# The output projection's last 1024 columns: a fourth pair by seven products, and the two token tiles moved into their seeded banks in a fixed order

## The chip, the cores and the metric

The kernel runs on one core of a Trainium2 chip. The metric is the device time of one execution in microseconds (us), the median of several runs. A core has five engines that work side by side and wait for one another through semaphores: TensorE (PE; its weight loads are listed as PEld), VectorE (DVE), ScalarE (ACT), GpSimd (POOL) and SyncE (SP), which here only issues transfers between device memory and the on-chip memory. TensorE adds its products up in accumulation banks, which VectorE and ScalarE read; a bank of 512 float32 columns by 128 rows is called a bank below.

## The reference, cut to what matters

One layer is computed (DEPTH is 1), for 256 tokens of width 2048, all in float32:

```python
h = rmsnorm(x, norm_g)
h, gate = adaln(h, c, ada_w, ada_b)          # shift, scale and gate from c
proj = h @ w_in                              # 2048 -> 4 x 4096
b_gate, c_gate, v, g = split(proj, 4)
u = causal_depthwise_conv(c_gate * v, conv_w)
y = b_gate * u * silu(g)                     # (256, 4096)
x = x + gate * (y @ w_out)                   # 4096 -> 2048
return rmsnorm(x, final_g)
```

The change concerns the product `y @ w_out`, 256 x 4096 times 4096 x 2048, and the gated residual and final norm behind it.

## The kernel before

**Precision.** Each float32 operand of a matmul is split in two parts: a high part, a cast made by ScalarE (`split_hi`, L352), and a low part, the rest, a subtraction made by VectorE (`split_lo`, L357). A product is then three matmuls, high x high, high x low and low x high (`triple`, L719). The 4096 rows of `w_out` are cut into 32 blocks of 128, taken two at a time: 16 *pairs*, numbered 0 to 15. The tokens are two *token tiles* of 128, t = 0 and 1. The split activations `y` stay on chip.

**Columns.** The 2048 output columns are done in two halves of 1024 (`columns`, L771), each in two blocks of W = 512. In a half, a pair is loaded as one tile of 128 x 2048 (1 MB, `load_o`) and used in one of two ways.

- A *direct* pair: 2 token tiles x 2 blocks of rows x 2 blocks of columns = 8 triples, 24 matmuls. It costs ScalarE one cast and VectorE one low part of 128 x 2048.
- A pair *by seven products* (`seven`, L736): the 2 x 2 x 2 block product in Winograd's form, 7 triples, 21 matmuls. Sums of the weight blocks are built on VectorE (L742, L744, L745), the raw blocks that are used are cast (L743) and their low part taken (L746), and the sums are split too (L352, L357). The matching sums of the activations (`forms`) were made earlier, for pairs 10 to 15 (`token_forms`), whether they are used once or twice. Four sums land in banks of their own (p1, p6 and the two of p75) and are put together after the last such pair (`gather`, L761 to L769).

In the first half all six pairs 10 to 15 go by seven products; in the second half three (10, 11, 12), between direct pairs. The list in the call sets the order of the pairs. Pairs 6 to 9 of the second half come last, in four pieces of a single block of columns: `LAST = (3, 4)` names two groups of four row blocks (pairs 6 and 7, pairs 8 and 9), first for columns 1024 to 1535 (the *third quarter*), then for columns 1536 to 2047 (the *fourth quarter*), 24 matmuls each.

**The seeded banks.** The fourth quarter's part that the pairs have summed up is moved before its end: for each token tile (L845 to L850) VectorE adds the bank and the gathered sums (L847), multiplies by the gate (L848) and adds the residual (L849), and ScalarE copies the result into another bank, `po[t]` (L850). The last two pieces of weights are multiplied by the gate before they are split (L862), so their products add straight onto the seeded bank: 48 matmuls, the last of the kernel. What follows for each token tile is a square with its sum (L877), a root (L818, with one load of ScalarE's function table), a reciprocal (L819), scalings on VectorE and ScalarE (L826, L824, L828) and four output transfers (L829). The sums of squares of the other columns (`part_sum`, L871 and L872) have to be there for the root.

**Buffers.** Three kinds of tiles of 128 x 2048 rotate over three places each: raw weights and weight sums (`raw_o`, `sums_o`), high parts (`hi`), low parts (`lo`). A pair by seven products takes two places of each kind in turn. A cast can start only when the matmuls that used the place three tiles ago are done, and a load is issued only when the last reader of its place is done: for a direct pair's tile that is its low part (L357), for a raw tile of the other form L746.

**Order.** The program is written as a plain sequence; a scheduler puts each engine's instructions into one queue, and an engine works through its queue strictly from front to back. `in_order()` pins the order of what is traced within it, `behind(ended)` puts instructions behind the last pinned ones. Around the change before, the order was left to the scheduler.

Of the kernel before, what the change touches and what calls it, by code (L numbers as in the profile page):

```python
# [11 lines left out]
ALU = mybir.AluOpType  # L12
# [7 lines left out]
TT = T // P  # L20
# [10 lines left out]
SLOT = 2048  # L31
# [86 lines left out]
def short_conv_layer(ctx: ExitStack, tc: tile.TileContext, x, c, norm_g, ada_w, ada_b, w_in, conv_w, w_out, final_g, out):  # L118
    nc = tc.nc
# [25 lines left out]
    def w_tile(kind, name, dtype=F32, i=None):  # L145

        if i is None:
            i = nth[kind] % 3
            nth[kind] += 1
        return wpool.tile([P, SLOT], dtype, tag=f"{kind}{i}", name=name, bufs=1)  # L150
# [9 lines left out]
    def raw_tile(name):  # L160
        return w_tile("raw", name)
# [3 lines left out]
    @contextmanager  # L165
    def in_order():

        traced = nc.cur_bb.bb.instructions
        n = len(traced)
        yield  # L170
        last = {}
        for ins in list(traced[n:]):
            if ins.engine in last:
                tc.add_manual_dep(ins, last[ins.engine], after, reason="in order")
            last[ins.engine] = ins.name
        ended.update(last)

    @contextmanager
    def behind(last):

        traced = nc.cur_bb.bb.instructions
        n = len(traced)
        yield
        for ins in list(traced[n:]):
            if ins.engine in last:
                tc.add_manual_dep(ins, last[ins.engine], after, reason="behind")
# [13 lines left out]
    ended = {}  # L200
# [75 lines left out]
    for t in range(TT):  # L276
        for dh in range(2):
# [3 lines left out]
            else:  # L281
                nc.vector.scalar_tensor_tensor(
                    out=junk[:, t], in0=xt[t][dh], scalar=1.0, in1=xt[t][dh], op0=ALU.mult, op1=ALU.mult,
# [60 lines left out]
    def hi_tile():  # L344
        return w_tile("hi", "hi", F32R)

    def lo_tile(lo_tag="lo"):
        return w_tile(lo_tag, "lo", F32R)

    def split_hi(raw, n, hi=None):  # L350
        hi = hi_tile() if hi is None else hi
        nc.scalar.copy(hi[:, :n], raw[:, :n])  # L352
        return hi

    def split_lo(raw, n, hi, lo_tag="lo", lo=None):
        lo = lo_tile(lo_tag) if lo is None else lo
        nc.vector.tensor_tensor(out=lo[:, :n], in0=raw[:, :n], in1=hi[:, :n].bitcast(F32), op=ALU.subtract)  # L357
        return hi, lo
# [13 lines left out]
    def split(raw, n, lo_tag="lo"):  # L372

        return split_lo(raw, n, split_hi(raw, n), lo_tag)
# [216 lines left out]
    def gate(dc):  # L591
        return gates[dc // 2][:, dc % 2, :]
# [36 lines left out]
    SEVEN = range(10, 16)  # L629
# [24 lines left out]
    for ct in range(NS, NCT, 2):  # L654
        for q in QUARTERS:
            bank = psum.tile([P, CT, T], F32, tag="mm", name="mm_b")[:, 0:2]
            col = q * E + ct * P
            for kp in range(0, KT, KP):
                raw = raw_tile("raw")
# [4 lines left out]
                hi, lo = split(raw, SLOT)  # L664
# [28 lines left out]
    W = 512  # L693
    big = hpool.tile([P, 3 * D + W], F32, tag="big", name="big")
    xr = big[:, 0 : TT * D].rearrange("p (t f) -> p t f", t=TT)
    fg = big[:, TT * D : 3 * D]
    u2 = big[:, 3 * D :]
    ends = [z.rearrange("p a b f -> p (a b f)").rearrange("p (h f) -> p h f", h=2) for z in zs]
# [11 lines left out]
    def load_o(raw, e0, ne, c0, n):  # L710
        nc.sync.dma_start(
            raw.rearrange("p (k f) -> p k f", k=ne),
            w_out[0, e0 * P : (e0 + ne) * P, c0 : c0 + n].rearrange("(k p) f -> p k f", p=P),
        )
# [9 lines left out]
    def gated(t, c0, n, src, pr, at):  # L724


        cs = slice(c0, c0 + n)
        r = xr[:, t, cs]
        g = gates[c0 // 1024].rearrange("p a f -> p (a f)")[:, c0 % 1024 : c0 % 1024 + n]
        nc.vector.tensor_tensor(out=pr, in0=src, in1=g, op=ALU.mult)  # L730
        nc.vector.tensor_tensor(out=r, in0=r, in1=pr, op=ALU.add)
        nc.scalar.activation(pr, r, AF.Square, scale=D**-0.5, accum_out=fsq[:, t, at : at + 1])
        nc.vector.tensor_tensor(out=r, in0=r, in1=fg[:, cs], op=ALU.mult)
# [37 lines left out]
    def columns(c0, order, sevens, bank, p1, p6, p75, whole, loads=None):  # L771


        for n, j in enumerate(order):
            raw = w_tile("raw" if n == 0 and c0 == 0 else "lo", "raw_o")
            load_o(raw, 2 * j, 2, c0, 2 * W)
            if loads:
                loads(n - 4)
            if j in sevens:
                seven(j, raw, bank, p1, p6, p75, j == sevens[0], j == sevens[-1])  # L780
                if j == sevens[-1]:
                    gather(p1, p6, p75)
                continue
            hi, lo = split(raw, SLOT, "raw")
            places = [(t, k, d) for t in range(TT) for k in range(2) for d in range(2)]
            if n == 0 and c0:
                places.sort(key=lambda p: p[2])
            for t, k, d in places:
                o = slice((k * 2 + d) * W, (k * 2 + d + 1) * W)
                triple(  # L790
                    bank(t, d), y_parts(2 * j + k, t), hi[:, o], lo[:, o],
                    n == 0 and k == 0, j == order[-1] and k == 1 and (whole or d == 1),
                )

    def extra_banks():
        return [psum.tile([P, W], F32, tag="sm", name="mm_1", bufs=2) for _ in range(2)]

    def wide_bank(name):
        return psum.tile([P, 2, W], F32, tag="mm", name=name)
# [7 lines left out]
    for t in range(TT):  # L807
        c = ends[t].rearrange("p h f -> p (h f)")
        nc.vector.tensor_tensor(out=c, in0=wide[t].rearrange("p h f -> p (h f)"), in1=c, op=ALU.add)
    for t in range(TT):  # L810
        c = ends[t].rearrange("p h f -> p (h f)")
# [3 lines left out]
    def finish(t):  # L815
# [15 lines left out]
    halves = [wide_bank("mm_o") for _ in range(2)]  # L831
    p75 = wide_bank("mm_7")
    LAST = (3, 4)
    po = extra_banks()
    columns(
        2 * W, (0, 1, 2, 10, 3, 13, 11, 4, 14, 12, 5, 15), SEVEN[0:3],
        lambda t, d: halves[d][:, t], *po, p75, False,
    )

    def out_mm(bank, t, ep, hi, lo):  # L840
        for i in range(EP):
            o = slice(i * W, (i + 1) * W)
            triple(bank, y_parts(ep * EP + i, t), hi[:, o], lo[:, o], False, ep == LAST[-1] and i == EP - 1)

    for t in range(TT):  # L845
        c = ends[t][:, 1]
        nc.vector.tensor_tensor(out=c, in0=halves[1][:, t], in1=c, op=ALU.add)  # L847
        nc.vector.tensor_tensor(out=c, in0=c, in1=gate(3), op=ALU.mult)  # L848
        nc.vector.tensor_tensor(out=c, in0=c, in1=xr[:, t, 3 * W : 4 * W], op=ALU.add)  # L849
        nc.scalar.copy(po[t], c)  # L850
    for ep in LAST:
        raw = w_tile("lo", "raw_o")
        load_o(raw, ep * EP, EP, 2 * W, W)
        hi, lo = split(raw, SLOT, "raw")
        for t in range(TT):
            out_mm(halves[0][:, t], t, ep, hi, lo)
    late = []
    for ep in LAST:
        raw = w_tile("lo", "raw_o")
        load_o(raw, ep * EP, EP, 3 * W, W)  # L860
        raw3 = raw.rearrange("p (k f) -> p k f", k=EP)
        nc.vector.tensor_tensor(out=raw3, in0=raw3, in1=gate(3).unsqueeze(1).to_broadcast([P, EP, W]), op=ALU.mult)  # L862
        hi, lo = split(raw, SLOT, "raw")
        out_mm(po[0], 0, ep, hi, lo)
        late.append((ep, hi, lo))
    for t in range(TT):
        c = ends[t][:, 0]
        nc.vector.tensor_tensor(out=c, in0=halves[0][:, t], in1=c, op=ALU.add)
        gated(t, 2 * W, W, c, c, 1)
        ps = part_sum[:, t : t + 1]  # L870
        nc.vector.reduce_sum(ps, fsq[:, t, 0:2], axis=mybir.AxisListType.X)  # L871
        nc.vector.tensor_scalar_add(ps, ps, EPS)  # L872
# [30 lines left out]
```

## Time and profile before

| | |
|---|---|
| time, median of 3 runs (lowest, highest) | 905.26 us (904.65, 905.49) |
| profiled execution: its own time | 905.34 us |
| its span, first to last instruction | 903.6 us |
| TensorE: matmuls busy, weight loads busy | 888.2 us (98%), 851.0 us (94%) |
| VectorE busy | 670.2 us (74%) |
| ScalarE busy | 482.4 us (53%) |
| GpSimd busy | 87.3 us (10%) |
| granted TensorE clock, mean | 0.998 |
| moved by the DMA engines | 235.01 MB, mean 260 GB/s |
| second half of the columns: first matmul | at 809.92 us |

Times in the profile are counted from the span's start. The span is a little shorter than the time of the execution, so a time read from the trace has to be carried over by differences. Matmuls are pipelined: a row's length is longer than the distance to the next matmul, and the distance is what counts. Rows of a time view give start, length, engine, line, operation, written tile <- read tiles, shape and count, and in brackets the idle time before with what ended it. Tiles are written without their number there.

### The profile page before, as it was taken

The numbers are of one execution on the slowest core, as the hardware profiler recorded it, in microseconds if no ns is written. First come the engines' busy times: TensorE is split into PE (matmuls) and PEld (weight loads), VectorE is DVE, ScalarE is ACT, GpSimd is POOL, SyncE is SP. The second block draws the span as 40 slices with busy tenths as digits, with TensorE's granted clock in tenths as the row PEclk, the third lists the DMA queues.
The fourth block names the chain that finished last, engine by engine and source line by source line (L and its number), as shares of the span: only waits on it lengthen the run. The fifth ranks groups of instructions, "written<-read, shape, count | busy, mean of one in ns | idle before, by whom it ended". The sixth has DMA issues, their size and how long they took to land.

```text
span 903.6 us, 16403 instructions
## 1 busy us (share of the span) xinstructions
PE 888.2 (98%) x7000; PEld 851.0 (94%) x7000; DVE 670.2 (74%) x661; ACT 482.4 (53%) x427; POOL 87.3 (10%) x95
## 2 busy tenths in 40 slices
PE   7999999999999999999999999999999999999996
PEld 4899999999999999999999999999999988888884
DVE  5889989888888867765875677565555578889685
ACT  6767866665548756644433434443434435544443
POOL 0000000000000132024324303320000000000000
PEclk9999999999999999999999999999999999999999
DMA  9999999999998587687988888866666486675652
GB/s 309 366 368 368 363 313 354 353 369 351 351 328 286 162 279 247 187 257 236 287 238 241 257 279 263 248 211 200 188 187 190 138 304 209 212 251 163 214 182 94
DMA packets 159594, 235.01 MB, mean 260 GB/s; under 512 B 6804, under 2 KB 105284, under 8 KB 159136
## 3 DMA queue, kind: packets, MB, share of 16 engines
q1 hardware_dynamic: 156384, 226.56, 76.7%
q0 software_dynamic: 3008, 7.34, 2.8%
q8 instruction: 55, 0.90, 0.4%
q14 instruction: 19, 0.16, 0.1%
q10 hardware_dynamic: 128, 0.04, 0.0%
HBM read 224.49 MB, written 2.10 MB: 251 GB/s over the span
## 4 chain that ended last, share of the span: by engine, by line
PE 90%; DMA 4%; DVE 2%; ACT 1%; SPq 1%; issue 1%; ACTq 0%
PE mm_b L491 39%; PE mm_s L491 36%; PE mm_w L722 7%; PE mm_o L722 5%; PE mm L722 4%; DMA at<-in_ada_w_dram 2%; DVE lo L357 1%; SPq L231 1%; DMA raw_s<-in_sc_w_in_dram 1%; ACT hi L352 1%; DMA x<-in_x_dram 1%; DMA raw_o<-in_sc_w_out_dram 1%; PE tp_g L481 0%; DVE raw_o L862 0%; ACT mm_s L524 0%
## 5 line engine op out<-in xcount | busy, mean ns | idle before, releaser
L491 PE MATMUL mm_s<-hT,hi 128*128 128x256 f32 x2048 | 350.3, 277 | 1.8 <-ACT hT L328 1.0
L491 PE MATMUL mm_b<-hT,hi 128*128 128x256 f32 x2048 | 348.2, 276 | 0.0
L491 PEld LDWEIGHTS mm_s<-hT,hi 128*128 128x128 f32 x2048 | 308.1, 188 | 2.4 <-ACT hT L328 1.2
L491 PEld LDWEIGHTS mm_b<-hT,hi 128*128 128x128 f32 x2048 | 308.6, 188 | 0.0
L491 PE MATMUL mm_b<-hT,lo 128*128 128x256 f32 x1024 | 282.6, 276 | 0.0
L491 PE MATMUL mm_s<-hT,lo 128*128 128x256 f32 x1024 | 282.0, 277 | 0.1
L357 DVE TENSOR_TENSOR lo<-raw,hi 128x2048 fp32r<-128x2048 f32 (+1 forms) x66 | 151.8, 2301 | 101.4 <-ACT hi L352 101.1
L352 ACT CAST hi<-raw 128x2048 fp32r<-128x2048 f32 (+1 forms) x66 | 123.7, 1875 | 191.6 <-PE mm_b L491 150.7
L491 PEld LDWEIGHTS mm_b<-hT,lo 128*128 128x128 f32 x1024 | 192.2, 188 | 0.0
L491 PEld LDWEIGHTS mm_s<-hT,lo 128*128 128x128 f32 x1024 | 191.7, 188 | 0.3 <-DVE lo L357 0.3
L357 DVE TENSOR_TENSOR lo<-raw_s,hi 128x2048 fp32r<-128x2048 f32 (+1 forms) x80 | 149.3, 1872 | 39.6 <-ACT hi L352 39.1
L352 ACT CAST hi<-raw_s 128x2048 fp32r<-128x2048 f32 (+1 forms) x80 | 123.9, 1557 | 56.1 <-PE mm_s L491 51.7
L474 DVE SCALAR_TENSOR_TENSOR gv<-at,silu_c,gv 128x512 f32<-128x512 f32 x105 | 78.6, 749 | 3.6 <-DMA at<-in_ada_w_dram 1.9
L512 ACT COPY acc<-mm_s 128x1024 f32<-128x1024 f32 x54 | 54.7, 1013 | 42.4 <-PE mm_s L491 42.3
L357 DVE TENSOR_TENSOR lo<-raw_o,hi 128x2048 fp32r<-128x2048 f32 x23 | 52.5, 2289 | 25.7 <-ACT hi L352 25.7
L352 ACT CAST hi<-raw_o 128x2048 fp32r<-128x2048 f32 x23 | 43.8, 1908 | 48.4 <-PE mm_o L722 17.3
L722 PE MATMUL mm_o<-hi,y 128*128 128x512 f32 x188 | 59.0, 389 | 0.0
L722 PE MATMUL mm_w<-hi,y 128*128 128x512 f32 x184 | 58.8, 389 | 0.0
L623 POOL TENSOR_TENSOR gacc<-gacc,z 128x512 f32<-128x512 f32 x28 | 45.9, 1639 | 119.3 <-DMA z<-gacc 119.3
L617 DVE SCALAR_TENSOR_TENSOR gacc<-at_g,silu_c,gacc 128x512 f32<-128x512 f32 x60 | 45.9, 764 | 8.0 <-DMA at_g<-in_ada_w_dram 6.9
L621 POOL DMA_DIRECT2D z<-gacc x28 | 15.7, 561 | 330.6 <-DVE acc L558 284.9
L722 PEld LDWEIGHTS mm_o<-hi,y 128*128 128x128 f32 x188 | 35.3, 188 | 7.3
(152 smaller groups left out, 675.4 us busy)
## 6 DMA issues: line engine op xcount, KB each, us to landing
raw<-in_sc_w_in_dram SPq DMA_DIRECT2D x64, 1024.0 KB, 5.8
raw_s<-in_sc_w_in_dram SPq DMA_DIRECT2D x47, 1024.0 KB, 7.7
raw_o<-in_sc_w_out_dram SPq DMA_DIRECT2D x32, 1024.0 KB, 5.2
at<-in_ada_w_dram SPq DMA_DIRECT2D x114, 256.0 KB, 7.8
raw_s<-in_sc_w_in_dram SPq DMA_DIRECT2D x33, 512.0 KB, 6.7
at_g<-in_ada_w_dram SPq DMA_DIRECT2D x32, 512.0 KB, 7.8
at<-in_ada_w_dram SPq DMA_DIRECT2D x6, 512.0 KB, 9.3
x<-in_x_dram SPq DMA_DIRECT2D x4, 512.0 KB, 6.2
```

What stands on the lines that cost most here:

```text
L231: nc.sync.dma_start(at[:, :, s, :], adas[:, j : j + kk, s, 0 : NK0 * P])
L352: nc.scalar.copy(hi[:, :n], raw[:, :n])
L357: nc.vector.tensor_tensor(out=lo[:, :n], in0=raw[:, :n], in1=hi[:, :n].bitcast(F32), op=ALU.subtract)
L474: nc.vector.scalar_tensor_tensor(out=gv, in0=at4[:, i], scalar=c_k, in1=gv, op0=ALU.mult, op1=ALU.add)
L491: mm = last_mm[0] = nc.tensor.matmul(dst, w, h[k], start=begins and left, stop=ends, skip_group_check=True)
L512: nc.scalar.copy(acc[ch, q], bank)
L617: nc.vector.scalar_tensor_tensor(out=ga, in0=at3[:, i, :], scalar=s, in1=ga, op0=ALU.mult, op1=ALU.add)
L621: nc.gpsimd.dma_start(turned[0 : P - away], ga[away:P])
L623: nc.gpsimd.tensor_tensor(out=ga, in0=ga, in1=turned, op=ALU.add)
L722: nc.tensor.matmul(dst, y[a], b, start=opens and i == 0, stop=ends and i == 2, skip_group_check=True)
```

## The change

Three edits, all in the second half of the columns.

1. Pair 13 goes by seven products as well (`SEVEN[0:4]` in place of `SEVEN[0:3]`), and the order of the pairs becomes 0, 1, 2, 10, 3, 11, 4, 12, 5, 13, 14, 15. Before, it was 0, 1, 2, 10, 3, 13, 11, 4, 14, 12, 5, 15.
2. The moves into the seeded banks are a function `move(t)`, and a pinned order is written: first gated piece, move of tile 0, its split, second gated piece, its cast, move of tile 1, its low part. The sums of the third quarter are put behind that (`behind(ended)`).
3. The matmuls of tile 0 on the last two pieces are traced after that block. Those of tile 1 stay where they were.

```diff
     columns(
-        2 * W, (0, 1, 2, 10, 3, 13, 11, 4, 14, 12, 5, 15), SEVEN[0:3],
+        2 * W, (0, 1, 2, 10, 3, 11, 4, 12, 5, 13, 14, 15), SEVEN[0:4],
         lambda t, d: halves[d][:, t], *po, p75, False,
     )
...
-    for t in range(TT):
+    def move(t):
         c = ends[t][:, 1]
         nc.vector.tensor_tensor(out=c, in0=halves[1][:, t], in1=c, op=ALU.add)
         nc.vector.tensor_tensor(out=c, in0=c, in1=gate(3), op=ALU.mult)
         nc.vector.tensor_tensor(out=c, in0=c, in1=xr[:, t, 3 * W : 4 * W], op=ALU.add)
         nc.scalar.copy(po[t], c)
...
-    late = []
-    for ep in LAST:
+    def gated_piece(ep):
         raw = w_tile("lo", "raw_o")
         load_o(raw, ep * EP, EP, 3 * W, W)
         raw3 = raw.rearrange("p (k f) -> p k f", k=EP)
         nc.vector.tensor_tensor(out=raw3, in0=raw3, in1=gate(3).unsqueeze(1).to_broadcast([P, EP, W]), op=ALU.mult)
-        hi, lo = split(raw, SLOT, "raw")
+        return raw
+
+    with in_order():
+        raw_a = gated_piece(LAST[0])
+        move(0)
+        late = [(LAST[0], *split(raw_a, SLOT, "raw"))]
+        raw_b = gated_piece(LAST[1])
+        hi_b = split_hi(raw_b, SLOT)
+        move(1)
+        late.append((LAST[1], *split_lo(raw_b, SLOT, hi_b, "raw")))
+    for ep, hi, lo in late:
         out_mm(po[0], 0, ep, hi, lo)
-        late.append((ep, hi, lo))
     for t in range(TT):
         c = ends[t][:, 0]
-        nc.vector.tensor_tensor(out=c, in0=halves[0][:, t], in1=c, op=ALU.add)
-        gated(t, 2 * W, W, c, c, 1)
+        with behind(ended):
+            nc.vector.tensor_tensor(out=c, in0=halves[0][:, t], in1=c, op=ALU.add)
+            gated(t, 2 * W, W, c, c, 1)
```

What the scheduler makes of it is seen at three places. The first is VectorE's queue from the direct pair 3 on. Before (pair 3's low part is `lo_8999`, pair 13's `lo_9029`, and pair 11 is the tile `raw_o_9055`):

```order
L357 TENSOR_TENSOR lo_8999<-raw_o_8995,hi_8997 128x2048
L357 TENSOR_TENSOR lo_9029<-raw_o_9025,hi_9027 128x2048
L742 TENSOR_TENSOR sums_o_9057<-raw_o_9055 128x1024
L744 TENSOR_TENSOR sums_o_9057<-raw_o_9055,sums_o_9057 128x512
L745 TENSOR_TENSOR sums_o_9057<-raw_o_9055,sums_o_9057 128x512
L746 TENSOR_TENSOR lo_9059<-raw_o_9055,hi_9058 128x1536
L357 TENSOR_TENSOR lo_9067<-sums_o_9057,hi_9065 128x2048
```

In the changed kernel pair 3 is `raw_o_8995` as before, pair 11 `raw_o_9025`, pair 4 `raw_o_9060`, pair 12 `raw_o_9090`, pair 5 `raw_o_9125` and pair 13 `raw_o_9155`:

```order
L742 TENSOR_TENSOR sums_o_9027<-raw_o_9025 128x1024
L357 TENSOR_TENSOR lo_8999<-raw_o_8995,hi_8997 128x2048
L744 TENSOR_TENSOR sums_o_9027<-raw_o_9025,sums_o_9027 128x512
L745 TENSOR_TENSOR sums_o_9027<-raw_o_9025,sums_o_9027 128x512
L746 TENSOR_TENSOR lo_9029<-raw_o_9025,hi_9028 128x1536
L357 TENSOR_TENSOR lo_9037<-sums_o_9027,hi_9035 128x2048
L742 TENSOR_TENSOR sums_o_9092<-raw_o_9090 128x1024
L357 TENSOR_TENSOR lo_9064<-raw_o_9060,hi_9062 128x2048
L744 TENSOR_TENSOR sums_o_9092<-raw_o_9090,sums_o_9092 128x512
```

For pairs 11 and 12 the first subtraction of the raw blocks (L742) now stands ahead of the low part of the direct pair before (3 and 4). For pair 13 it stands behind the low part of pair 5.

The second place is VectorE's queue at the moves; `z_4470` holds token tile 0's sums, `z_4471` token tile 1's. Before:

```order
L862 TENSOR_TENSOR raw_o<-raw_o,gate_4469 128x2048
L357 TENSOR_TENSOR lo<-raw_o,hi 128x2048
L862 TENSOR_TENSOR raw_o<-raw_o,gate_4469 128x2048
L847 TENSOR_TENSOR z_4470<-mm_o,z_4470 128x512
L847 TENSOR_TENSOR z_4471<-mm_o,z_4471 128x512
L357 TENSOR_TENSOR lo<-raw_o,hi 128x2048
L848 TENSOR_TENSOR z_4470<-z_4470,gate_4469 128x512
L848 TENSOR_TENSOR z_4471<-z_4471,gate_4469 128x512
L357 TENSOR_TENSOR lo<-raw_o,hi 128x2048
L849 TENSOR_TENSOR z_4470<-z_4470,big 128x512
L849 TENSOR_TENSOR z_4471<-z_4471,big 128x512
```

Now (the three lines of the move are L855 to L857, the gated product is L864):

```order
L864 TENSOR_TENSOR raw_o<-raw_o,gate_4469 128x2048
L855 TENSOR_TENSOR z_4470<-mm_o,z_4470 128x512
L856 TENSOR_TENSOR z_4470<-z_4470,gate_4469 128x512
L857 TENSOR_TENSOR z_4470<-z_4470,big 128x512
L357 TENSOR_TENSOR lo<-raw_o,hi 128x2048
L864 TENSOR_TENSOR raw_o<-raw_o,gate_4469 128x2048
L855 TENSOR_TENSOR z_4471<-mm_o,z_4471 128x512
L856 TENSOR_TENSOR z_4471<-z_4471,gate_4469 128x512
L857 TENSOR_TENSOR z_4471<-z_4471,big 128x512
L357 TENSOR_TENSOR lo<-raw_o,hi 128x2048
```

Tile 0's move is now complete ahead of the first gated piece's low part, and tile 1's ahead of the second's; before, the last step of both stood behind both low parts.

The third place is TensorE's queue among the last 48 matmuls; `mm_8868` is token tile 0's seeded bank, `mm_8869` token tile 1's, `y_4444` and `y_4457` the activations of the first piece, `y_4460` and `y_4461` those of the second:

```order
 L722 MATMUL mm_8869<-hi,y_4457 128x512
 L722 MATMUL mm_8869<-hi,y_4460 128x512
+L722 MATMUL mm_8868<-lo,y_4460 128x512
+L722 MATMUL mm_8868<-hi,y_4460 128x512 x2
+L722 MATMUL mm_8868<-lo,y_4460 128x512
+L722 MATMUL mm_8868<-hi,y_4460 128x512
+L722 MATMUL mm_8868<-hi,y_4461 128x512
+L722 MATMUL mm_8868<-lo,y_4461 128x512
+L722 MATMUL mm_8868<-hi,y_4461 128x512 x2
+L722 MATMUL mm_8868<-lo,y_4461 128x512
+L722 MATMUL mm_8868<-hi,y_4461 128x512
 L722 MATMUL mm_8869<-lo,y_4460 128x512
```

Before, tile 0 had all its 24 matmuls first. Now tile 1's twelve of the first piece (and the first of the second) stand ahead of tile 0's last eleven.

More of the change, by code (lines that the diff above doesn't have):

```diff
@@ L843, in out_mm @@
             triple(bank, y_parts(ep * EP + i, t), hi[:, o], lo[:, o], False, ep == LAST[-1] and i == EP - 1)
-    for t in range(TT):
[L846 to L850, printed above, removed]
     for ep in LAST:
@@ L856, in short_conv_layer @@
             out_mm(halves[0][:, t], t, ep, hi, lo)
-    late = []
-    for ep in LAST:
+    def move(t):
+        c = ends[t][:, 1]
+        nc.vector.tensor_tensor(out=c, in0=halves[1][:, t], in1=c, op=ALU.add)
+        nc.vector.tensor_tensor(out=c, in0=c, in1=gate(3), op=ALU.mult)
+        nc.vector.tensor_tensor(out=c, in0=c, in1=xr[:, t, 3 * W : 4 * W], op=ALU.add)
+        nc.scalar.copy(po[t], c)
+    def gated_piece(ep):
         raw = w_tile("lo", "raw_o")
```

## The prediction

> **What bounds the kernel now.** I read the chain that ended last first, then the busy time by stretches, then the order of time of the last 80 us, engine by engine. The chain by engine, and its last pieces (start us, length us, what):
>
> ```profile
> PE 90%; DMA 4%; DVE 2%; ACT 1%; SPq 1%; issue 1%; ACTq 0%
> ...
> 883.54 0.61 DVE z L849
> 884.15 0.02 issue
> 884.18 0.60 ACT mm L850
> 884.78 0.04 issue
> 884.82 11.23 PE mm L722 x48
> 896.05 0.02 issue
> 896.07 0.70 ACT z L877 x2
> ```
>
> TensorE is the bound for nine tenths of the span. Only at the end does the chain pass to VectorE: the last sum of the move (L849) and, on ScalarE, the copy into the bank (L850) release the last 48 matmuls, and their end releases the square of token tile 1 (L877), behind which the outputs follow. Busy time in stretches (stretch, length, then PE, PEld, DVE, ACT, POOL, clock, DMA share, GB/s):
>
> ```profile
> 840.00:860.00 20.00, 20.00 (x90) 16.57 (x89) 11.96 (x9) 9.27 (x6) 0.00 (x0) 1.00 0.68 222
> 870.00:880.00 10.00, 10.00 (x45) 8.27 (x45) 9.96 (x6) 3.23 (x2) 0.00 (x0) 1.00 0.27 98
> ```
>
> While the pairs run (840 to 860) VectorE has 8 us in 20 free; from 870 it has none. So this change touches three places: the count of matmuls, VectorE's queue at 826 to 855, and the last 20 us.
>
> **The pace, and term 1: three matmuls fewer.**
>
> ```profile
> 830.61 0.84 PE L722 MATMUL mm_o<-hi,y 128*128 128x512 f32 x3
> ...
> 883.65 0.39 PE L722 MATMUL mm_o<-hi,y 128*128 128x512 f32 x1
> 884.82 0.50 PE L722 MATMUL mm<-hi,y 128*128 128x512 f32 x1 [0.79 <-ACT mm L850]
> ...
> 895.65 0.39 PE L722 MATMUL mm<-hi,y 128*128 128x512 f32 x1
> ```
>
> From 830.61 (the last matmul of pair 10) to 883.65 (the last one for the third quarter of the columns) lie 234 matmuls (two pairs of 21, eight of 24): 53.04 / 234 = 0.2267 us, the pace I use. 884.82 is the first of the last 48 (fourth quarter), 895.65 the last. Pair 13 falls from eight triples to seven: 3 x 0.2267 = 0.68 us less.
>
> **Term 2: the stall ahead of the last 48.** Without it they would start at 883.65 + 0.23 = 883.88 and end 48 x 0.2267 = 10.88 us later, at 894.76; their last slot ends at 895.65 + 0.23 = 895.88. Lost: 1.12 us (0.94 idle, the rest slower first matmuls). In the new order VectorE does tile 0's move right after the first gated piece. I follow that queue from the cast for the second piece of the third quarter (LAST's pair of pairs 8 and 9), which waits for pair 14's end, 72 slots = 16.3 us before that quarter's last matmul. With that end near 883.9 (below): pair 14 done 867.8, cast to 869.7, low part to 872.0; gated product 2.2, to 874.2; three steps of tile 0's move at 0.60, to 876.0; copy into the bank to 876.6; cast of the gated piece to 878.5, its low part to 880.8. So the last 48 find their bank and both operands 3 us early, and the stall goes. What is late next: second product to 883.0, tile 1's move to 884.8, its copy to 885.4, needed after 13 slots, at 886.9: 1.5 us of cover; the second low part is done at 887.1 and needed after 26 slots, at 889.8. Cover gone, each us late costs a us.
>
> **Term 3: a new wait at pair 4.** For pairs 11 and 12, VectorE's queue now has the subtraction of the raw block (L742) ahead of the low part of the direct pair before it. Rows for durations and for the load that stands first:
>
> ```profile
> 750.01 2.29 DVE L357 TENSOR_TENSOR lo<-raw_o,hi 128x2048 fp32r<-128x2048 f32 x1 [0.98 <-ACT hi L352]
> 752.22 1.22 DVE L742 TENSOR_TENSOR sums_o<-raw_o 128x1024 f32<-128x1024 f32 x1
> 753.47 0.69 DVE L744 TENSOR_TENSOR sums_o<-raw_o,sums_o 128x512 f32<-128x512 f32 x1
> 754.20 0.69 DVE L745 TENSOR_TENSOR sums_o<-raw_o,sums_o 128x512 f32<-128x512 f32 x1
> 754.81 1.75 DVE L746 TENSOR_TENSOR lo<-raw_o,hi 128x1536 fp32r<-128x1536 f32 x1
> ...
> 760.21 2.29 DVE L357 TENSOR_TENSOR lo<-raw_o,hi 128x2048 fp32r<-128x2048 f32 x1 [0.97 <-ACT hi L352]
> ...
> 821.79 0.37 SPq L711 DMA_DIRECT2D raw_o<-in_sc_w_out_dram  x1
> ...
> DMA to landing us min/median/max: 5.4/5.4/5.4
> ...
> DMA to landing us min/median/max: 5.0/5.1/6.7
> ```
>
> The first landing line is that of the load issued at 821.79 (pair 13's before, pair 11's now), the second that of all the loads from 780 on. In the first half of the columns the low part stood first, and one direct pair and one by seven products took 760.21 - 750.01 = 10.2 us, 45 matmuls at PE's pace: no wait. Now: pair 11 lands at 827.2; L742 to 828.4; the low part of pair 3 starts 1.13 in, at 828.35, to 830.6 (PE needs it at 831.3: no wait). L744 830.55, L745 831.27, L746 831.9 to 833.6. That frees the buffer for pair 12's load, issued 833.65, landed 838.75 (at 5.1). L742 waits for it, though the low part of pair 4 could start once pair 3 has ended and its cast is done (836.7 + 1.9 = 838.6). So that low part runs from 839.9 to 842.2. PE comes to it 49 slots after 830.61, at 841.72. Stall 0.5 us; with a landing of 5.4, 0.8; the restart cost 0.18 in the row of 884.82. I take s = 0.75, range 0 (landing 4.6 or less) to 2.2 (6.7, plus restart). Behind it PE's own lateness gives VectorE back time, and for pair 13 the low part stands first again: no second stall at 5.1 to 5.4. VectorE's net 4.3 us more (L742 to L746 at 1.25 + 0.72 + 0.61 + 1.67) fall into the free 40% of 840 to 860; ScalarE's 1.48 too. SP issues as many loads as before, each when its buffer frees.
>
> The Trainium skill ("DMA: Bandwidth & Descriptors", section "Anatomy of one DMA — SWDGE (gpsimd) path") fits a transfer as 2.0 us plus its bytes at 436 GB/s. For these 1 MB that is 4.4 us as an estimate, and by it s would be 0 and the time that of the first rival. The trace says 5.0 at least, and it decides; the fit was made on another path than the one in use here.
>
> **Term 4: token tile 0's own end.** The new PE order is: tile 0's first 12, tile 1's first 12 and then the rest. Counting its rows, tile 0's last matmul is slot 12 + 1 + 12 + 1 + 11 = 37 of 48 instead of 24. ScalarE has one queue, and in it tile 0's square, table load, root and two scalings (L818, L828) stand ahead of tile 1's square:
>
> ```profile
> 890.69 0.60 ACT L877 ACTIVATE z<-mm 128x512 f32<-128x512 f32 x1 [1.57 <-PE mm L722]
> 891.19 0.19 ACT L877 ACTIVATION_READ_ACCUMULATOR z<-mm 128x1 f32 x1
> 891.40 1.28 ACT L818 ACT_TABLE_LOAD   x1
> 892.70 0.30 ACT L818 ACTIVATE fs<-fsq,part_sum 128x1 f32<-128x1 f32 x1
> 893.22 1.34 ACT L828 ACTIVATE big<-big,fs 128x512 f32<-128x512 f32 x2 [0.23 <-DVE fs L819]
> 896.07 0.60 ACT L877 ACTIVATE z<-mm 128x512 f32<-128x512 f32 x1 [1.51 <-PE mm L722]
> ...
> 884.67 1.28 DVE L868 TENSOR_TENSOR z<-mm_o,z 128x512 f32<-128x512 f32 x2
> ...
> 889.88 0.27 DVE L872 TENSOR_SCALAR part_sum<-part_sum 128x1 f32<-128x1 f32 x2
> ```
>
> From 890.69 to 893.22 + 1.34 = 894.56 ScalarE is taken for 3.87 us; before, that ended 1.5 us ahead of tile 1. Now the last 48 start at 883.88 - 0.68 + s = 883.20 + s. Tile 0's square starts 37 x 0.2267 + 0.18 (drain of the last matmul, 0.39 - 0.23, and 0.02) = 8.57 later, and tile 1's 3.87 after that: at 895.64 + s. PE would allow it at 883.20 + s + 10.88 + 0.18 = 894.26 + s. Tile 0's end therefore takes the path, by 1.4 us. The part sums that the table load waits for took VectorE from 884.67 to 889.88 + 0.27, 5.5 us; now they begin after its second low part (887.1, above) and end at 892.6, while tile 0's square ends at 893.3: covered by 0.7 us. Tile 0's outputs leave 1.8 us later, still ahead of tile 1's.
>
> **Sum.** Tile 1's square: 896.07 before, 895.64 + 0.75 = 896.39 now: +0.32 us. What follows it is unchanged: 903.6 - 896.07 = 7.53 us, so the span is 903.9. Around the span lie 905.34 - 903.6 = 1.74 us; the profiled execution stands 0.08 above the median of 905.26. 905.26 + 0.32 = 905.6 us. In short, -0.68 and -1.12 on PE, +0.75 at pair 4, +1.38 at tile 0's end. A difference below 0.2% (1.8 us) can't be told from no change here.
>
> **The rivals.**
>
> No wait at pair 4: the load lands before L742 would hold anything up. For it: a gain of 0.5 us is enough. Against: no load in the trace landed under 5.0. Time: s = 0, 905.26 - 0.43 = 904.8.
>
> A late load for pair 12 (slower): the place is L742 of pair 12 ahead of pair 4's low part; it decides from a landing of 4.6 us on, a us for a us. For it: landings of up to 6.7 stand in the trace. Against: their median is 5.1. At 6.7: s = 2.2, +1.8, 907.0 us; if pair 13's load is late too, its first matmul, which stands early in pair 5, waits for the cast and adds 1 us.
>
> PE's end decides: tile 1's square isn't behind tile 0's end, so the path is 894.26 + 0.75 = 895.0, -1.06, 904.2 us. For it: the chain before ran through PE. Against: the queue order, and ScalarE has no second queue.
>
> The change doesn't do what it says: the moves come late after all, since VectorE is full from 870, and the stall of 1.12 stays beside the rest: 905.6 + 1.1 = 906.7. Against: 7 us between tile 0's copy and its use.
>
> **How the numbers follow.** Forecast (s of 0.5 to 1.1) 0.63, own range 905.2 to 906.2; no wait 0.13; late load 0.14; PE's end 0.04; moves late 0.04; nothing of these 0.02. Taking in both kinds of s and half of the 0.8 us by which the runs of before spread: 904.5 to 907.0. Slower by over 0.2% needs more than 1.8 us: half of the late load and a little besides, 0.08. Faster by over 0.2% has no case above, 0.03 for what I have missed. Within 0.2%: 0.89.
>
> **What would show it.** Right: PE idle about 0.5 to 0.8 us before a matmul with pair 4's low part, near 842; no idle time before the last 48; tile 0's square near 892.5 and tile 1's right behind L828, not released by PE. Wrong: PE full from 831 to the last matmul (term 3), a wait on the bank's copy (term 2), or tile 1's square released by PE (term 4). A time under 904.3 or over 907.2 would mean that a term is missing.

## The result and the profile after

| | before | after |
|---|---|---|
| time, median (lowest, highest), 21 runs each | 905.49 us (904.65, 910.29) | 907.39 us (905.81, 909.33) |
| ratio, 95% interval | | 1.0018 (1.001 to 1.0025) |
| profiled execution, its span | 905.34, 903.6 us | 906.79, 905.0 us |
| granted TensorE clock, mean | 0.998 | 0.997 |

The change costs 0.1 to 0.25%, where no difference was forecast (905.6, range to 907.0). By the profile the loss lies in the last 75 us. TensorE's work is the same in both kernels up to the last matmul of pair 10, so I count from that row (830.61 before, 830.17 after) and leave out what the two executions differed by until there, 0.44 us.

| counted from pair 10's last matmul | before | after | moved | forecast |
|---|---|---|---|---|
| first of the last 48 matmuls | +54.21 | +53.97 | -0.24 | -0.87 |
| tile 1's square | +65.46 | +66.46 | +1.00 | +0.32 |
| end of the span | +72.99 | +74.83 | +1.84 | +0.32 |

The matmul rows of after, by time, that carry the table and the stall:

```profile
830.17 0.84 PE L722 MATMUL mm_o<-hi,y 128*128 128x512 f32 x3
...
842.53 0.50 PE L722 MATMUL mm_o<-lo,y 128*128 128x512 f32 x1 [1.09 <-DVE lo L357]
...
884.14 0.39 PE L722 MATMUL mm<-hi,y 128*128 128x512 f32 x1
```

There is no idle time before 884.14: the stall ahead of the last 48 is gone. In its place stands one at pair 4's low part. From 830.17 to the first of the last 48 are now 232 slots, 52.59 us at 0.2267; it starts at +53.97, so the stall, with the slower matmuls right behind it, costs 1.38 us. The chain of waits of after shows what the low part came from (start, length, what):

```profile
827.82 2.29 DVE lo L357
...
831.44 1.68 DVE lo L746
833.12 0.02 issue
833.14 5.81 DMA raw_o<-in_sc_w_out_dram
...
839.11 1.08 issue
840.19 2.30 DVE lo L357
842.49 0.04 issue
842.53 2.56 PE mm_o L722 x10
```

Read from the bottom: pair 4's low part (840.19) stood in the queue behind pair 12's first subtraction; that waited for pair 12's load (5.81 us); and the load waited for its buffer, which L746 of pair 11 freed. From one direct pair's low part to the next VectorE takes 840.19 - 827.82 = 12.37 us by this way; TensorE needs 45 x 0.2267 = 10.2.

The tail on ScalarE and the end of VectorE's part sums, in order of time:

```profile
892.79 0.60 ACT L889 ACTIVATE z<-mm 128x512 f32<-128x512 f32 x1 [0.20 <-PE mm L722]
893.28 0.19 ACT L889 ACTIVATION_READ_ACCUMULATOR z<-mm 128x1 f32 x1
893.57 1.28 ACT L818 ACT_TABLE_LOAD   x1
...
896.63 0.57 ACT L889 ACTIVATE z<-mm 128x512 f32<-128x512 f32 x1
```

```profile
885.92 2.29 DVE L357 TENSOR_TENSOR lo<-raw_o,hi 128x2048 fp32r<-128x2048 f32 x1
...
893.34 0.27 DVE L884 TENSOR_SCALAR part_sum<-part_sum 128x1 f32<-128x1 f32 x2
```

Tile 1's square (896.63) has no release by TensorE any more: it starts when ScalarE is done with tile 0, 3.84 us after tile 0's square. The table load (893.57) needs tile 0's part sum, the first of the two steps in the last row, which is done less than 0.1 us ahead of it.

Last, the busy time by stretches of 1 us at the end (the last two columns are DMA share and GB/s), after and then before:

```profile
896.00:897.00 1.00, 0.00 (x0) 0.00 (x0) 0.54 (x1) 1.00 (x3) 0.00 (x0) 1.00 0.22 86
897.00:898.00 1.00, 0.00 (x0) 0.00 (x0) 0.31 (x2) 0.74 (x4) 0.00 (x0) 1.00 1.07 397
898.00:899.00 1.00, 0.00 (x0) 0.00 (x0) 1.00 (x2) 1.00 (x2) 0.00 (x0) 1.00 1.07 367
899.00:900.00 1.00, 0.00 (x0) 0.00 (x0) 0.00 (x1) 0.19 (x1) 0.00 (x0) 0.77 1.03 381
900.00:901.00 1.00, 0.00 (x0) 0.00 (x0) 0.00 (x0) 0.00 (x0) 0.00 (x0) 0.50 1.08 393
```

```profile
896.00:897.00 1.00, 0.04 (x1) 0.00 (x0) 0.00 (x0) 0.90 (x3) 0.00 (x0) 1.00 1.07 363
897.00:898.00 1.00, 0.00 (x0) 0.00 (x0) 0.84 (x3) 0.77 (x3) 0.00 (x0) 1.00 0.44 150
898.00:899.00 1.00, 0.00 (x0) 0.00 (x0) 0.47 (x1) 0.65 (x2) 0.00 (x0) 1.00 0.32 125
899.00:900.00 1.00, 0.00 (x0) 0.00 (x0) 0.00 (x0) 0.00 (x0) 0.00 (x0) 0.93 1.07 406
```

Before, tile 0's four outputs were all but through when tile 1's began (the last one lands at 898.30, tile 1's first is issued at 897.83): the DMA share falls to 0.44 and 0.32 in between. After, the engines are full from 897 to 901, since tile 0's outputs are issued only 2.5 us ahead of tile 1's (before 4.1). From tile 1's square to the end of the span it takes 8.37 us (905.0 - 896.63) instead of 7.53: another 0.84 us. Two things are in it. The last output lands 3.7 us after its issue in place of 3.1, and tile 1's four issues lie 0.3 us farther apart: the second comes 0.77 us behind the first in place of 0.44, as the issue rows show (after, then before):

```profile
898.37 0.33 SPq L829 DMA_DIRECT2D out_dram<-big  x1
899.14 0.33 SPq L829 DMA_DIRECT2D out_dram<-big  x1
```

```profile
897.83 0.33 SPq L829 DMA_DIRECT2D out_dram<-big  x1
898.27 0.37 SPq L829 DMA_DIRECT2D out_dram<-big  x1
```

### The profile page after: what moved, and what is told of

The parts are those of the page before. It is cut to its first block, busy times and chain, and to the rows that moved or that the text cites. A ratio compares the mean times of both kernels' runs of the same rounds, so it can differ in the third digit from the quotient of the medians.

```text
span 905.0 us, 16403 instructions
## 1 busy us (share of the span) xinstructions
PE 887.3 (98%) x6997; PEld 850.5 (94%) x6997; DVE 674.9 (75%) x665; ACT 484.0 (53%) x428; POOL 89.4 (10%) x95
## 4 chain that ended last, share of the span: by engine, by line
PE 87%; DMA 4%; DVE 3%; ACT 2%; SPq 1%; issue 1%; ACTq 0%; DVEq 0%
PE mm_b L491 38%; PE mm_s L491 36%; PE mm_w L722 7%; PE mm_o L722 3%; PE mm L722 2%; DMA at<-in_ada_w_dram 2%; DVE lo L357 1%; DMA raw_o<-in_sc_w_out_dram 1%; ACT hi L352 1%; DMA raw_s<-in_sc_w_in_dram 1%; SPq L231 1%; DMA x<-in_x_dram 1%; DVE raw_o L864 0%; PE tp_g L481 0%; ACT big L828 0%
## 5 line engine op out<-in xcount | busy, mean ns | idle before, releaser
L357 DVE TENSOR_TENSOR lo<-raw_o,hi 128x2048 fp32r<-128x2048 f32 x22 | 50.4, 2290 | 23.1 <-ACT hi L352 23.1
L623 POOL TENSOR_TENSOR gacc<-gacc,z 128x512 f32<-128x512 f32 x28 | 49.9, 1782 | 129.6 <-DMA z<-gacc 129.6
L722 PE MATMUL mm_o<-hi,y 128*128 128x512 f32 x176 | 55.2, 389 | 0.0
L722 PEld LDWEIGHTS mm_w<-hi,y 128*128 128x128 f32 x184 | 34.5, 188 | 7.1
```

The costliest lines, as they stand in the source:

```text
L623: nc.gpsimd.tensor_tensor(out=ga, in0=ga, in1=turned, op=ALU.add)
L722: nc.tensor.matmul(dst, y[a], b, start=opens and i == 0, stop=ends and i == 2, skip_group_check=True)
```

## The experiments

Every kernel was timed against the kernel before on its own chip; "before" below is that median. Distances "+" are counted from pair 10's last matmul, as above.

**Edit 1 alone.**

```diff
-        2 * W, (0, 1, 2, 10, 3, 13, 11, 4, 14, 12, 5, 15), SEVEN[0:3],
+        2 * W, (0, 1, 2, 10, 3, 11, 4, 12, 5, 13, 14, 15), SEVEN[0:4],
```

> Only the first edit: pair 13 by seven products and the new order of the pairs; the tail's code is that of the kernel before, and the scheduler now puts both moves' first steps ahead of the gated pieces' low parts. Theory (the stall at pair 4 and tile 0's end with colliding outputs cost the time, the stall before the last 48 goes by itself): PE idle 0.5 to 1.3 us at pair 4, none before the last 48, tile 1's square released by ScalarE's own queue, outputs back to back at the end; span 0.9 to 1.9 us above the kernel before. Rival (the pinned order of edit 2 is what costs the time): the span is below the kernel before, by 0.4 us or more, since three matmuls are gone.

906.46 us (before 905.14), ratio 1.0017 (1.0007 to 1.0027). The wait at pair 4 is there without the pinned order:

```profile
842.36 0.50 PE L722 MATMUL mm_o<-lo,y 128*128 128x512 f32 x1 [0.76 <-DVE lo L357]
```

The loss comes with edit 1. Tile 1's square is released by ScalarE's own queue and the outputs meet, as the theory had it; the span is 0.6 us above that of before, less than its 0.9 to 1.9. And there is no stall ahead of the last 48 (+53.68) although the moves are left to the scheduler. The wait at pair 4 gives them time here, but the same holds further down without that wait: edit 1 takes the stall away too.

**Edits 2 and 3 alone**, with the pairs as before.

> Only the second and third edits, with the pairs of the kernel before (three by seven products, the old order). Theory: no idle time at pair 4; the stall of 1.1 us before the last 48 goes; tile 0's square comes 8.6 us after their start instead of 5.9, its table load waits for the part sums until about 893, tile 1's square starts 0.2 to 0.4 us later than before, and the outputs collide for 0.8 us more: +0.8 to +1.3 us in all. Rival (the stall at pair 4 is the whole loss, the tail's new order a gain of 1.1 us): -1.1 us.

905.76 us (before 905.14), ratio 1.0006 (0.9997 to 1.0015). No idle time at pair 4 nor ahead of the last 48 (+53.27, which is 235 slots x 0.2267). ScalarE's rows:

```profile
893.28 1.28 ACT L818 ACT_TABLE_LOAD   x1 [0.22 <-DVE part_sum L884]
...
896.34 0.57 ACT L889 ACTIVATE z<-mm 128x512 f32<-128x512 f32 x1
```

A stall of 1.1 us is gone and the time is not better: tile 1's square, at +65.88, is 0.4 later than before, behind tile 0's end. Here the table load waits for the part sums as well. The median is 0.6 us above before, short of the 0.8 to 1.3 expected, and its interval takes in no change; the rival's gain of 1.1 us is outside the interval.

**The low part first.** The changed kernel, with the first subtraction of pairs 11 to 13 pinned behind the low part of the direct pair before (`low_part[0]` holds that instruction).

```diff
-        nc.vector.tensor_tensor(out=s[:, 0:2], in0=b[:, 1:3], in1=b[:, 0:1].to_broadcast([P, 2, W]), op=ALU.subtract)
+        before_it = low_part[0]
+        first_sums = nc.vector.tensor_tensor(out=s[:, 0:2], in0=b[:, 1:3], in1=b[:, 0:1].to_broadcast([P, 2, W]), op=ALU.subtract)
+        if not whole and j > 10:
+            tc.add_manual_dep(first_sums.ins, before_it.ins.name, after, reason="the low part before comes first")
```

> The changed kernel with one order put back: for pairs 11, 12 and 13 the first subtraction of the raw blocks stands behind the low part of the direct pair before it on VectorE. Theory: the 1.25 us of idle time and slow restart at pair 4 go, everything behind it comes 1.2 to 1.4 us earlier, tile 0's end and the outputs stay as they are: 1.2 to 1.4 us faster than the changed kernel, within 0.6 us of the kernel before. Rival (VectorE's tail, not PE, sets the end, since the part sums release the table load): the idle time goes, but the end moves by less than 0.4 us.

905.35 us (before 905.14), ratio 1.0003 (0.9994 to 1.0012). No idle time on TensorE from 826 on, first of the last 48 at +52.78, against +53.97: 1.2 us, the wait at pair 4 and its restart. Of the 2.1 us of span, 0.2 lie ahead of pair 10's last matmul and 0.7 at the end (7.66 us behind tile 1's square, not 8.37).

**The same pinning on edit 1 alone.**

> Edit 1 alone, with the first subtraction of pairs 11 to 13 behind the low part of the direct pair before; the moves and the matmuls of the last 48 as before the change. It tells what edits 2 and 3 are worth once the wait at pair 4 is gone. First theory (they are worth nothing or a little less, since edit 1 takes the stall ahead of the last 48 away by itself and tile 0's end on ScalarE sets tile 1's square either way): first of the last 48 at 882.7 to 883.0, tile 1's square at 894.8 to 895.3, span 902.5 to 903.0, time 904.8 to 905.3, within 0.5 us of the same pinning with edits 2 and 3 (905.35 in its run). Rival (edits 2 and 3 take a stall away): idle time ahead of the last 48, time 906 or more.

905.46 us (before 905.4), ratio 1.0003 (0.9994 to 1.0012): the same as with edits 2 and 3. No idle time, first of the last 48 at +52.61, tile 1's square at 894.84 behind tile 0's end. Once the pairs are in the new order, edits 2 and 3 bring nothing.

**Tile 0 first.** The changed kernel, with the 24 matmuls of tile 0 ahead of those of tile 1 in the last 48 (`tile_0` is the last one of tile 0).

```diff
-                out_mm(po[1], 1, ep, hi, lo)
+                with behind({tile_0.ins.engine: tile_0.ins.name}):
+                    out_mm(po[1], 1, ep, hi, lo)
```

> The changed kernel with tile 0's 24 matmuls ahead of tile 1's 24 on PE, as in the kernel before. First theory (tile 0's place among the 48 is the cause of its late end): its square at about 889.9 instead of 892.8, its outputs about 2.9 us earlier, tile 1's square released by PE at about 895.2, 1.4 us earlier, and no collision of outputs: 2.2 us faster than the changed kernel. Second theory (the part sums are as late as tile 0's square, since the pinned order puts the third quarter's sums behind everything): the square is earlier, but the table load still starts at about 893.5 and the end moves by less than 0.3 us.

907.21 us (before 905.14), ratio 1.002 (1.0011 to 1.0029): no gain. TensorE and then ScalarE:

```profile
887.94 0.50 PE L722 MATMUL mm<-lo,y 128*128 128x512 f32 x1 [1.00 <-DVE lo L357]
```

```profile
890.83 0.60 ACT L892 ACTIVATE z<-mm 128x512 f32<-128x512 f32 x1 [4.61 <-PE mm L722]
...
893.71 1.28 ACT L819 ACT_TABLE_LOAD   x1 [0.98 <-DVE part_sum L886]
...
896.78 0.57 ACT L892 ACTIVATE z<-mm 128x512 f32<-128x512 f32 x1
```

Tile 0's square comes 2 us earlier and the table load does not: it waits for the part sums, which the pinned order puts behind the second low part. That low part, needed 12 slots earlier now, also stops TensorE for 1.00 us.

**Without tile 0's outputs**, to price the collision.

```diff
-            nc.sync.dma_start(out[t * P : (t + 1) * P, dd], r)
+            if t == 1:
+                nc.sync.dma_start(out[t * P : (t + 1) * P, dd], r)
```

> The changed kernel without token tile 0's four output transfers: those 256 KB pieces of the output are not written. It measures the collision of the two tiles' outputs by itself. First theory (tile 0's outputs, now issued 895.9 to 897.3, are still moving when tile 1's are issued from 898.4 on): from tile 1's square to the span's end the row falls from 8.37 us to the 7.5 of the kernel before, and the time from 907.4 to about 906.5; up to tile 1's square nothing moves (896.6). Rival (the longer end comes from something else, such as the issue of the transfers or the scalings): the end stays 8.2 to 8.4 us behind the square and the time within 0.2 us of the changed kernel's.

906.4 us (before 905.4), ratio 1.0011 (1.0002 to 1.002). TensorE idles at pair 4 as in the changed kernel (0.99 us), tile 1's square is at +66.28, and the span ends 904.3 - 896.91 = 7.39 us behind it, as the first theory forecast. But the run takes away more than the collision. Of the 1.0 us less, 0.5 are the landing of the last output (3.25 us after its issue, not 3.74), 0.3 the second issue of tile 1, which follows the first after 0.41 us again, and 0.2 a shorter stretch from the last landing to the end (0.97 us in place of 1.2). The late second issue is not shown to come from the collision: it comes after 0.75 to 0.77 us in all nine kernels that have edit 1 and write all outputs, also in the last of the two versions below, where the outputs hardly meet, and after 0.44 us with edits 2 and 3 alone, where they do. Its cause is not shown. So the collision by itself is worth about 0.5 us here.

**Both waits taken away, in two ways.** The first is the changed kernel with the low part first, tile 0 first, and another pinned order; the second is edit 1 with the low part first and tile 0 first, and no pinned order at the moves.

```diff
         raw_a = gated_piece(LAST[0])
-        move(0)
-        late = [(LAST[0], *split(raw_a, SLOT, "raw"))]
+        hi_a = split_hi(raw_a, SLOT)
         raw_b = gated_piece(LAST[1])
+        move(0)
         hi_b = split_hi(raw_b, SLOT)
+        late = [(LAST[0], *split_lo(raw_a, SLOT, hi_a, "raw"))]
+        late.append((LAST[1], *split_lo(raw_b, SLOT, hi_b, "raw")))
         move(1)
-        late.append((LAST[1], *split_lo(raw_b, SLOT, hi_b, "raw")))
```

> Both waits taken away and tile 0 ended early: the changed kernel with the first subtraction of pairs 11 to 13 behind the low part of the direct pair before, the 24 matmuls of tile 0 ahead of those of tile 1, and the pinned order changed to both gated pieces, move of tile 0, both low parts, move of tile 1. First theory (four terms: three matmuls fewer, no stall, tile 1's square released by TensorE, no collision of outputs): no idle time on TensorE from 826 on, first of the last 48 matmuls at 882.7 to 882.9, tile 1's square at 893.8 to 894.4, end 7.5 to 7.7 us behind it, span 901.4 to 902.0, time 903.2 to 903.8. Rival (the move of tile 1 or the part sums still come too late, so that ScalarE's end of tile 0 sets tile 1's square as before): square at 895 or later, span 902.6 or more, time 904.8 to 905.4, as in the run with the low parts first.

904.65 us (before 905.4), ratio 0.9994 (0.9985 to 1.0003). The rival's picture: no stall, but tile 1's square at 895.07, because tile 0's end starts late:

```profile
892.01 1.28 ACT L824 ACT_TABLE_LOAD   x1 [0.98 <-DVE part_sum L892]
```

> Edit 1 alone, with the first subtraction of pairs 11 to 13 behind the low part of the direct pair before, and the 24 matmuls of tile 0 ahead of those of tile 1; no pinned order at the moves. First theory (the pinned order of the moves is not needed, since pair 13 by seven products takes the stall ahead of the last 48 away by itself): first of the last 48 at 882.7 to 883.0, part sums done by 889.5, tile 1's square released by TensorE at 893.8 to 894.4, span 901.4 to 902.0, time 903.2 to 903.8, as the run with the reordered block. Rival (without the pinned order a move comes late and the last 48 wait): idle time on TensorE ahead of them, square 0.5 to 1.5 us later, time 904 to 905.2.

904.12 us (before 905.4), ratio 0.9987 (0.9979 to 0.9996): faster than the kernel before by 0.04 to 0.21%, and by the ratios than the changed one, which was not timed beside it. ScalarE and one stretch of 1 us:

```profile
889.55 1.28 ACT L824 ACT_TABLE_LOAD   x1
...
894.22 0.60 ACT L885 ACTIVATE z<-mm 128x512 f32<-128x512 f32 x1 [1.51 <-PE mm L724]
```

```profile
896.00:897.00 1.00, 0.00 (x0) 0.00 (x0) 0.61 (x1) 0.80 (x2) 0.00 (x0) 1.00 0.18 72
```

The part sums are done by 889.3 (the row of L879 starts at 889.00), tile 1's square is released by TensorE again, at +63.84 (before +65.46), and the outputs hardly meet (the last of tile 0 lands at 896.35, tile 1's first is issued at 895.98). That is term 1 and term 2 of the prediction without terms 3 and 4: 1.62 us at the square. The end stands 7.88 us behind it, 0.35 more than before (0.3 of it the late second issue), so 1.3 us are left, short of the 1.6 to 2.2 expected.

**The code packet.** In the queues' table a packet of kind instruction (0.02 MB, queue 8) comes every 28 to 30 us of matmuls in before and after. In the changed kernel one falls right into pair 4's load (issued 830.14), which lands after 6.3 us, and pair 12's, 3.0 us behind, after 5.8. In the same trace two other loads 3.0 us apart (issued 842.50 and 845.50) have no packet in them and land after 5.0 and 5.1. Queue rows and loads of the stretch 829.9 to 832:

```profile
q8 instruction: 1, 0.02, 6.5%
...
raw_o<-in_sc_w_out_dram SPq DMA_DIRECT2D x1, 1024.0 KB, 6.3
```

To move the packet, filler matmuls near 9 us (their result is not used) were made more and narrower, first 6 more, then 15.

```diff
-    def idle(n):
+    def idle(n, w=512):
...
-            nc.tensor.matmul(tp_idle, ident, ones[:, 0:1].to_broadcast([P, 512]), start=True, stop=True)
+            nc.tensor.matmul(tp_idle[:, 0:w], ident, ones[:, 0:1].to_broadcast([P, w]), start=True, stop=True)
...
-    idle(IDLE[1])
+    idle(IDLE[1] + 6, 232)
```

> The changed kernel; only the filler matmuls near 9 us, whose result nobody reads, are 11 of 232 columns in place of 5 of 512 (each is two in the trace), so that TensorE has 24 instructions more in its queue, weight loads counted, and everything else keeps its order. In the trace a code packet (queue 8, kind instruction, 0.02 MB) comes about every 28.5 us, 126 matmuls with as many weight loads; in the changed kernel one stands at 831.2, inside the load for pair 4 (issued 830.14), which lands after 6.3 us; every load that takes 6.0 us or more there has such a packet inside it (800, 830, 859), and the load right behind it 5.5 to 5.9. First theory (the code packet holds the load up): 24 instructions earlier is 24 x 0.1133 = 2.7 us earlier, so the packet falls at about 828.5, between two loads; pair 4's load lands after 5.0 to 5.3 us and pair 12's after 5.0 to 5.3, TensorE's idle time at pair 4 falls from 1.09 to 0.3 to 0.5 us, and the time from 907.4 to about 906.6. Rival (the load is late for its place in the program, or for the overlap with the load 3.0 us behind it): 6.0 to 6.4 and 5.5 to 5.9 again, idle time 1.0 to 1.2 us, time 907.2 to 907.6.

906.41 us (before 905.44), ratio 1.0006 (0.9996 to 1.0016). The packet stands at about 826 (further forward than worked out), ahead of the loads of pairs 4 and 12, and they land after 5.4 and 5.3 us. Pair 4's load, and the matmul that waits for its low part:

```profile
raw_o<-in_sc_w_out_dram SPq DMA_DIRECT2D x1, 1024.0 KB, 5.4
```

```profile
842.14 0.50 PE L722 MATMUL mm_o<-lo,y 128*128 128x512 f32 x1 [0.53 <-DVE lo L357]
```

The idle time falls from 1.09 to 0.53 us. The first of the last 48 comes at +53.41, so the stall costs 0.82 us, against the 0.75 that the prediction took, and tile 1's square comes 0.36 us later than before, against +0.32. The first theory holds, against place in the program and overlap, both of which are unchanged here, though landing and idle time stand a little above its ranges. By the time alone it would not be shown: the interval overlaps that of the changed kernel (1.001 to 1.0025). And "every load that takes 6.0 us or more" is too much said: in the changed kernel the load issued at 789.42 takes 6.0 with no packet in it.

> As the run with 6 fillers more, with 15 more (20 of 128 columns in place of 5 of 512), so 60 instructions more in TensorE's queue. First theory: the code packet comes 60 x 0.1133 = 6.8 us earlier, at about 824.4, inside the load for pair 11 (issued near 821.4), which lands after 6.0 to 6.5 us instead of 5.2; that of pair 4 lands after 5.0 to 5.3. Pair 11's first subtraction, and with it the chain of VectorE up to the issue of pair 12's load, comes about 1 us later, so the idle time moves: 0.2 to 0.6 us at pair 3's low part near 831, and at pair 4 0.8 to 1.2 us less what pair 3 has already cost; time 906.8 to 907.6. Rival: pair 11's load 5.0 to 5.3 us, pair 4's 6.0 to 6.4, idle time at pair 4 alone, 1.0 to 1.2 us.

908.01 us (before 905.44), ratio 1.0022 (1.0008 to 1.0037). The run does not test what it was made for. TensorE's first products already start 0.9 us later (25.68 against 24.75), the later parts stand 2 to 4 us later, and the packet (at 824) falls just ahead of pair 11's load instead of into it. The loads of pairs 11, 4 and 12 have no packet in them and land after 5.2, 5.0 and 5.0 us, which speaks against the rival too; but two earlier loads took 6.4 and 7.5 us with no packet in them, while two loads were under way at once. So a packet is one cause of a late load and not the only one. TensorE idles at pair 3 (0.55 us) and at pair 4 (1.01 us), although the loads are quick: pair 11's load was issued late, and the way from one low part to the next is 11.5 us (831.69 to 843.22) even so, 1.3 us over TensorE's 10.2.

## Why the prediction was wrong in size and right in most steps

**Term 1, three matmuls fewer: right.** In the kernels without a stall the first of the last 48 comes at +52.61 to +52.99 with the new pairs, and at +53.27 with the old ones: 0.3 to 0.7 us earlier, where 0.68 was worked out.

**Term 2, the stall of 1.12 us goes: right, but it was given to the wrong edit alone.** It goes with edits 2 and 3 alone, and just as well with edit 1 alone. VectorE's queue was followed in one order only. Of the 1.5 us of cover for tile 1's bank 0.3 are left in after: its copy ends at 886.55 and is needed 12 slots after 884.14.

**Term 3, a new wait at pair 4: the mechanism right, the price too small.** "I take s = 0.75"; it was 1.38. Place, cause and queue are those of the prediction, and so is the issue of pair 12's load (3.04 us after pair 10's last matmul worked out, 2.97 measured). The step that failed is "landed 838.75 (at 5.1)": it landed after 5.8. The rest of the term holds: 0.5 us at 5.1, a us for a us above it, and 0.18 for the restart give 1.4 at 5.8. The sum took the median of all loads for this one. What it passed over is the code packet, which in the profile of before falls between two loads (between 831.5 and 831.8) and in the new order into pair 4's, with pair 12's right behind. It could have been read in the profile of before: there the two loads from 780 on that had a packet well inside them took 6.3 and 6.7 us, and the second is the 6.7 of the prediction's late load. With the packet elsewhere the idle time was 0.53 us. The Trainium skill's fit ("DMA: Bandwidth & Descriptors", section "Anatomy of one DMA — SWDGE (gpsimd) path"), 4.4 us as an estimate, is below every load of `w_out` in these traces (4.8 us at least).

**Term 4, tile 0's end ahead of tile 1's square: right, but for the cover.** Tile 0's square comes 8.65 us after the first of the last 48 (8.57 worked out), tile 1's 3.84 after that (3.87). "Covered by 0.7 us", of the part sums, was too much: in after they are done less than 0.1 us ahead, in edits 2 and 3 alone the table load waits 0.22 us for them, and with tile 0 first 0.98. So term 4 had a second cause ready behind the first.

**The step priced at nothing: "Tile 0's outputs leave 1.8 us later, still ahead of tile 1's", and "What follows it is unchanged".** Counted from pair 10, tile 0's leave 2.6 us later and tile 1's 1.0 us later, and the two sets meet. The forecast compared the issues, which do keep their order, and not the landings. Its own figures had it: the first issues, 4.1 us apart before, come to stand 4.1 - 1.8 + 0.3 = 2.6 us apart, while tile 0's four outputs took 4.6 us from the first issue to the last landing (893.74 to 898.30). In the profile the end behind the square costs 0.84 us, more than the miss of term 3 (0.63): some 0.5 to 0.6 the meeting, 0.3 the late second issue, whose cause stays open. The price of the meeting varies: the last output lands 3.0 to 3.7 us after its issue, mean 3.4, in the nine profiles where the outputs meet, and 3.1 to 3.3 in the three where they hardly do or there is one set alone.

Together: +0.32 forecast, 0.68 more up to tile 1's square and 0.84 behind it make the +1.84 of the profile. Of the rivals, the late load came nearest; it forecast a landing of 6.7 and so covered by luck what the outputs took. The profiled execution of after is 1.45 us slower than that of before, the median 1.9 us: this 0.45, and why the runs of after spread over 3.5 us, most of them above the profiled one, is not shown. The kernel with no wait and hardly a collision spreads over 0.9 us (903.84 to 904.75).

## What to carry to other kernels

Where a loop alternates two kinds of steps, write down for each order how long one engine's queue takes from one step to the same step of the next round, loads included, and compare it with the bound engine's round: here 11.5 to 12.5 us against 10.2 in the new order, and no wait once the low part stood first. For a load on that way, look in the trace for what else the DMA queues carry while it is under way, and do not take the median of all loads. A late finish is not priced by the order of issues: transfers that used to be alone need to be laid, from issue to landing, over those that they will now meet. A fix for a stall is worth trying on its own, since another edit of the same change may already remove it; the version that won here, edit 1 with two orders pinned elsewhere, has none of edits 2 and 3.

## What the runs showed of the hardware that was not expected

- A code packet of 0.02 MB that starts at least 1 us into a load of 1 MB, and at least 1 us ahead of its landing, goes with a landing of 6.0 to 7.0 us in place of about 5.1: so in 29 of the 31 such loads behind 780 us in the twelve profiles, 5.5 us in the other two. A packet in a load's last microsecond does not (5.0 to 5.4 us). The load issued some 3.0 us behind lands after 5.5 to 6.4 us. Moving the packet by fillers took it out of the way (6.3 to 5.4 us). Loads of 6.0 us and more without a packet stand there too, nine of 164, and how a packet holds a load up is not shown.
- At the end of after the second tile's output transfers were issued at 898.37, 899.14, 899.57 and 900.07, and took 2.7, 3.1, 3.6 and 3.7 us to land, and the last of these issues itself took 1.34 us on SP in place of some 0.4 (row 900.07). DMA shares of 1.03 to 1.08 stand in the rows of 897 to 901. The long issue is not what made the landing late: with 6 fillers more the last issue took 0.41 us and its output landed after 3.6.
- Three dependent steps of 128 x 512 on VectorE come 0.72 us apart (882.41, 883.13, 883.85 in the run with the low part first); pairs of independent ones are 0.60 apart (two from 886.75 to 887.95). The prediction had taken 0.60 for both.
